# One encoder layer on one core: the per-layer-input product moved into two-bank PSUM tiles, and two norm chains joined into one

## The chip, the cores and the metric

The kernel runs on one core of one Trainium2 chip, as one launch. The metric is device time in microseconds (us) from start to end of an execution, lower is better. The times shown are those of single runs; the profile is one execution recorded by the hardware profiler.

## The reference

One layer of a streaming encoder is computed for 1024 prompt frames and 32 sample frames, in float32. The part that this change touches is the end of the mixing block, the start of the feed-forward block and the per-layer input:

```python
x = x + rms_norm(mix @ w_out, g_post_mix)            # W_out, post-mix norm
hf = rms_norm(x, g_pre_ffn)                          # pre-FFN norm
a, u = split(hf @ w_up, 2)                           # W_up: 1024 x 5632
ffn = (gelu(causal_conv3(a)) * u) @ w_down
x = x + rms_norm(ffn, g_post_ffn)
x = x + (p @ w_ple) * sigmoid(x @ w_ple_gate)        # "ple": p is 256 wide, w_ple 256 x 1024
```

`rms_norm(x, g)` is `x * rsqrt(mean(x*x) + 1e-6) * g` over the 1024 features of a token.

## The kernel before, in words

All 1056 tokens are kept feature-major: 128 partitions hold 128 features, and the tokens lie along the free dimension. In the stages of interest the tokens are cut in four groups of 264 (`H`); groups 0 and 1 are token pair 0, groups 2 and 3 token pair 1. A float32 product is made of three fast products (`product`, L200 to L202): weights and data are each split in a rounded high part and the remainder, and high x high, high x low and low x high are summed in PSUM. ScalarE (ACT) makes the high part with a copy, VectorE (DVE) the low part with a subtraction. A block is one output tile of 128 features x 264 tokens.

The stages around the change, in the order in which TensorE (PE) runs them:

- **W_out** (loop over `p`, then `c`): for each pair, eight output blocks per group, each 24 matmuls. `z_out` copies a finished block out of PSUM and squares it (ACT), and DVE adds the squares into `sqz[g]`. While pair 1 runs, pair 0 is finished beside it: its post-mix norm, its residual sum `x1`, the squares of `x1` (`x1_squares`, L1358 last), and the seven operands of its later products (`build_ops`, L1376 and L1377).
- **ple**: `ple_product` makes 32 blocks of 6 matmuls each (four groups, eight feature blocks `c`). Its PSUM tiles come from `mm_bank`, a ring of six single banks; each block is copied out on ACT (L1420) into an SBUF tile `x4` that takes four blocks, and GpSimd (POOL) issues the store of that tile to `ple_d` (L1422). There are three `x4` buffers, so the first copy into a buffer waits until the store made from it three tiles earlier has landed. Beside the blocks, a table `beside` (filled by `at(m, ...)`) issues pair 1's finishing work: the norm's rows, `x1_sum` on DVE (L1332, L1333), `x1_gain` on ACT (L1339, 16 instructions), operand casts on ACT (L1376) with their low parts on DVE (L1377).
- **up** (`up_unit`, 22 units): products of W_up by a seven-multiplication scheme on 2x2 blocks. Three PSUM tiles `X`, `Y`, `Z` of two banks each (tag `st`, a ring of three in the pool `pf`), one bank per half of the tokens. In unit 0 the two pairs run one after the other, seven steps of 12 matmuls each; the squares of pair 1 (L1362, ACT), their sums (L1367 to L1370, DVE) and its pre-FFN norm lie beside it. In the later units both pairs run in each step. Each step's PSUM result is read by one ACT or DVE operation (L1676 to L1694), and the next step that writes that tile waits for the reading.

A norm is a chain: `sums88` sums the squares over the partitions with tiny matmuls against a column of ones (L1305; three per group, seen as six passes), DVE computes the reciprocal root with a dozen operations on a few columns (`rsqrt`, L211 to L217), `norm_rows` spreads the result back over the partitions with six matmuls (L301, seen as 12 passes), and ACT copies it to `rbT` (L303). Pair 0's pre-FFN chain runs in W_out (sums at `c == 6`, rows after `c == 7`), pair 1's post-mix chain at the start of ple.

The order on each engine is set by the Tile scheduler from the program order, except that `behind(E)` and the like pin an instruction after the last one issued on that engine. Each engine works its own queue strictly in that order. PSUM has eight banks: two for `tr_bank` (tags `tr`) and six that first serve `mm_bank` (pool `pq`) and after ple the pool `pf`.

Of the kernel before, what the change touches and what calls it, by code (L numbers as in the profile page):

```python
# [10 lines left out]
F32 = mybir.dt.float32  # L11
F32R = mybir.dt.float32r
I32 = mybir.dt.int32
AF = mybir.ActivationFunctionType
ALU = mybir.AluOpType
AX = mybir.AxisListType

P = 128
D = 1024
# [3 lines left out]
EPS = 1e-6  # L23
# [7 lines left out]
H = 264  # L31
# [3 lines left out]
T88 = ((0, 88), (88, 88), (176, 88))  # L35
# [24 lines left out]
def layer_kernel(  # L60
# [7 lines left out]
    PSUM = bass.MemoryType.PSUM  # L68
# [9 lines left out]
    def nm(s):  # L78
        n_names[0] += 1
        return f"{s}_{n_names[0]}"  # L80
# [5 lines left out]
    V, S, G, E = nc.vector, nc.scalar, nc.gpsimd, nc.tensor  # L86

    def behind(*engines):

        st = ExitStack()  # L90
        for e in engines:
            ins = next(i for i in reversed(nc.cur_bb.bb.instructions) if i.engine == e.engine)
            st.enter_context(tc.issue_after(ins))
        return st
# [100 lines left out]
    def product(ps, w, wsl, xh, xl, ks, first=True, last=True):  # L195

        for n, (kw, kx) in enumerate(ks):
            wh, wl = w[0][:, kw, wsl], w[1][:, kw, wsl]
            a, b = xh[kx], xl[kx]
            E.matmul(ps, wh, a, start=first and n == 0, stop=False)  # L200
            E.matmul(ps, wh, b, start=False, stop=False)  # L201
            E.matmul(ps, wl, a, start=False, stop=last and n == len(ks) - 1)  # L202
# [1 line left out]
    ALL = slice(0, P)  # L204
    KS = tuple((k, k) for k in range(KT))

    def rsqrt(pool, out, v, n):

        bits = pool.tile([P, n], I32, tag="rsb", name=nm("rsb"), bufs=2)
        t = pool.tile([P, n], F32, tag="rst", name=nm("rst"), bufs=2)  # L210
        V.tensor_scalar(bits[:], v.bitcast(I32), 1, None, op0=ALU.logical_shift_right)  # L211
        V.tensor_scalar(bits[:], bits[:], -1.0, float(0x5F3759DF), op0=ALU.mult, op1=ALU.add)
        y = bits[:].bitcast(F32)
        for _ in range(3):
            V.scalar_tensor_tensor(t[:], y, -0.5, y, op0=ALU.mult, op1=ALU.mult)
            V.tensor_tensor(t[:], t[:], v, op=ALU.mult)
            V.scalar_tensor_tensor(out, t[:], 1.5, y, op0=ALU.add, op1=ALU.mult)  # L217
            y = out
# [19 lines left out]
    def tr_bank():  # L238
        return bank(pp, "tr", 2)
# [56 lines left out]
    def norm_rows(rs, tiles, out):  # L296

        n = sum(m_ for _, m_ in tiles)
        t = tr_bank()
        for i, (c, m_) in enumerate(tiles):  # L300
            E.matmul(t[:, c:c + m_], rs[:m_, i:i + 1].to_broadcast([m_, P]), ident[:m_, :m_],  # L301
                     start=True, stop=True)
        S.copy(out, t[:, :n])  # L303
# [7 lines left out]
    with right("ap") as ap:  # L311
# [210 lines left out]
        with tc.tile_pool(name="np", bufs=1, side="right", reuse_waits="tile") as np_:  # L522
# [103 lines left out]
            xt, rs, rb = ([], [], []), [], []  # L626
# [181 lines left out]
    with right("bp") as bp:  # L808
# [284 lines left out]
        def at(m, f, *a):  # L1093
            small.setdefault(m, []).append(lambda: f(*a))
# [78 lines left out]
    with right("mp") as mp:  # L1173
# [23 lines left out]
        def block(w, wsl, xh, xl, ks, n):  # L1197
            b = mm_bank()
            product(b[:, :n], w, wsl, xh, xl, ks)
            return b  # L1200
# [99 lines left out]
    def sums88(t, g, sq):  # L1300

        for i in range(3):
            o = t[:88, 3 * (g % 2) + i:3 * (g % 2) + i + 1]
            for k, q in enumerate(sq):
                E.matmul(o, q[:, 88 * i:88 * i + 88], ones[:], start=k == 0, stop=k == len(sq) - 1)  # L1305

    def pair_norm(p, scale, t=None, late=False):

        sums = t is None
        t = t or tr_bank()  # L1310
        v = fo.tile([P, 6], F32, tag="nv", name=nm("nv"), bufs=2)
        rs = fo.tile([P, 6], F32, tag="nr", name=nm("nr"), bufs=2)
        V.memset(v[:], 1.0)
        for g in (2 * p, 2 * p + 1) if sums else ():
            sums88(t, g, [sqz[g]])
        V.tensor_scalar(v[:88], t[:88, 0:6], scale, EPS, op0=ALU.mult, op1=ALU.add)
        rsqrt(fo, rs[:], v[:], 6)

        def rows():
            for h in range(2):  # L1320
                o = H * (2 * p + h)
                norm_rows(rs[:, 3 * h:3 * h + 3], T88, rbT[:, o:o + H])
        if sums and not late:
            rows()
        return rows
# [86 lines left out]
    def ple_product(g, beside):  # L1412
        xs = pT.pop(g)
        for c in range(8):
            if c % 4 == 0:
                t = oz.tile([P, 4, H], F32, tag="x4", name=nm("ple"), bufs=3)
            b = block(ple_w[c // 4], slice((c % 4) * P, (c % 4 + 1) * P),
                      [xs[:, 0, k, :] for k in range(2)], [xs[:, 1, k, :] for k in range(2)],
                      ((0, 0), (1, 1)), H)
            S.copy(t[:, c % 4, :], b[:, :H])  # L1420
            if c % 4 == 3:
                gdma(ple_d[:, c - 3:c + 1, H * g:H * g + H], t[:])  # L1422
            for f in beside.pop(8 * g + c, ()):
                f()
# [99 lines left out]
    for p in range(2):  # L1524
        for c in range(8):
            if p and c == 5:
                load_ple()
            w = next_w(2)
            for g in (2 * p, 2 * p + 1):
                z_out(c, g, block(w, ALL, Ra[g], Rb[g], KS, H))  # L1530
                if p == 0 and (c, g) != (0, 0):
                    next(early, None)
            if p == 0:
                if c == 6:
                    x_load(0)
                continue
            if c == 0:
                pair_norm(0, 0.25 / D)
                x1_part(0)
            if c == 1:  # L1540
                x1_squares(0)
                x_load(1)
                x1_part(1)
                op0 = build_ops(0)
            if 2 <= c < 6:
                next(op0)
            if c == 4:
                x1_squares(1)
                p_load(0)
                p_load(1)  # L1550
            if c == 6:
                for _ in op0:
                    pass
                x_load(2)
                x_load(3)
                with behind(E):
                    rows = pair_norm(0, 1.0 / D, late=True)
                p_load(2)
                p_load(3)
            if c == 7:  # L1560
                with behind(E):
                    rows()

    for i in range(4):
        load_part(i)
    rows = pair_norm(1, 0.25 / D, late=True)
    beside = {}

    def at(m, f, *a, on=()):
# [9 lines left out]
        return z[g][:, 4 * i:4 * i + 4, :].bitcast(F32)  # L1579

    b11, b21, b12, b22 = q_rows(2, 0), q_rows(2, 1), q_rows(3, 0), q_rows(3, 1)
    at(6, rows, on=(E,))
    for n, (g, i) in enumerate(((2, 0), (2, 1), (3, 0), (3, 1))):
        at(7, x1_sum, g, i)
        for h in range(2):
# [14 lines left out]
    octx.close()  # L1600
    fctx = ExitStack()
    fp = fctx.enter_context(right("fp"))
    qctx.close()
    qctx = ExitStack()
    pf = qctx.enter_context(tc.tile_pool(name="pf", bufs=1, space=PSUM, reuse_waits="tile"))
    us0 = fp.tile([P, T + 2], F32, tag="a", name="us0", bufs=2)[:, 0:T]
    Sp = page(lq, 3, [P, 4, 2, H], "Sp")
    s1c, U2, nU3, t12 = (Sp[:, i].bitcast(F32) for i in range(4))
# [335 lines left out]
```

## Time and profile before

| | |
|---|---|
| runs | 2012.38, 2012.46 and 2016.8 us; median 2012.46 us |
| profiled execution, span from first to last instruction | 2012.8 us |
| PE busy | 1985.5 us, 99% of the span |
| DVE, ACT, POOL busy | 71%, 48%, 11% |
| TensorE clock, mean of the span | 0.996 of full |

The profiled execution is 0.3 us longer than the median of the runs, so its rows can be set against the runs as they are. In the timeline a row's first number is its start in us from the span's start and the second its duration; matmuls are pipelined, so each is shown for about 0.28 us while the next one starts 0.12 us later. A bracket at a row's end gives how long the engine had been idle and what ended that. W_out's last blocks, ple and unit 0 of up lie between 1150 and 1221 us.

### The profile page before, as it was taken

Reading aid. Unit: us, or ns where it says so; the run is one execution under the profiler, and the core shown is the slowest. Engines: PE = TensorE matmul, PEld = TensorE weight load, DVE = VectorE, ACT = ScalarE, POOL = GpSimd, SP = SyncE. Lnnn points to the kernel's source line nnn. Section 1 sums busy time; section 2 is a strip of 40 time slices with the busy share of each in tenths; the row PEclk is TensorE's granted clock in tenths of the full one; section 3 lists DMA queues with packets and bytes.
Section 4 is the critical chain, followed back from the end, with each engine's and each line's share of the span. In section 5 each row is a group of like instructions: output and inputs, shape, how many; then the busy total and the mean of one; then the engine's idle time right before and its main releaser. Section 6 shows DMA issues by size and latency. Waiting matters only on the chain.

```text
span 2012.8 us, 37342 instructions
## 1 busy us (share of the span) xinstructions
PE 1985.5 (99%) x14282; PEld 1955.1 (97%) x14282; DVE 1433.6 (71%) x3193; ACT 965.6 (48%) x2184; POOL 226.2 (11%) x318
## 2 busy tenths in 40 slices
PE   7999999999999999999999999999999999999998
PEld 6999999999999999999999999999999999999998
DVE  5788888688888888554455778788887884655552
ACT  5655566556666666542124763333333344444432
POOL 2010100000000000002001123332333310000000
PEclk8999999999999999999999999999999999999999
DMA  8322321411111111377558582222222246655542
GB/s 263 96 94 68 115 64 53 144 54 57 37 54 37 54 53 56 118 229 230 165 167 291 164 296 64 85 75 85 68 92 65 88 137 202 214 190 172 167 129 82
DMA packets 250807, 245.31 MB, mean 122 GB/s; under 512 B 13365, under 2 KB 218696, under 8 KB 250629
## 3 DMA queue, kind: packets, MB, share of 16 engines
q1 hardware_dynamic: 242085, 214.92, 34.2%
q0 software_dynamic: 8464, 27.94, 3.9%
q8 instruction: 112, 1.84, 0.4%
q14 instruction: 66, 0.54, 0.1%
q10 hardware_dynamic: 80, 0.07, 0.0%
HBM read 177.56 MB, written 65.32 MB: 121 GB/s over the span
## 4 chain that ended last, share of the span: by engine, by line
PE 85%; DVE 5%; issue 2%; DMA 1%; ACT 1%; POOL 1%; SPq 0%; POOLq 0%; ACTq 0%; DVEq 0%
PE mm L200 13%; PE mm L201 13%; PE mm L202 13%; PE st L1667 7%; PE st L1665 7%; PE st L1666 7%; PE G L839 2%; PE Y L836 2%; PE G L838 2%; PE G L836 2%; PE Y L839 2%; PE Y L838 2%; PE tr L469 1%; PE X L836 1%; PE so L1030 1%
## 5 line engine op out<-in xcount | busy, mean ns | idle before, releaser
L1665 PE MATMUL st<-op,wt 128*128 128x264 f32 x1232 | 349.1, 284 | 3.7 <-ACT ple L1420 2.3
L1667 PE MATMUL st<-op,wt 128*128 128x264 f32 x1232 | 350.2, 284 | 0.0
L1666 PE MATMUL st<-op,wt 128*128 128x264 f32 x1232 | 348.4, 283 | 0.0
L184 DVE TENSOR_TENSOR wl<-wr,wh 128x1024 fp32r<-128x1024 f32 x132 | 161.6, 1225 | 129.3 <-ACT wh L181 115.5
L1665 PEld LDWEIGHTS st<-op,wt 128*128 128x128 f32 x1232 | 231.8, 188 | 4.8 <-ACT ple L1420 2.5
L1666 PEld LDWEIGHTS st<-op,wt 128*128 128x128 f32 x1232 | 232.1, 188 | 0.0
L1667 PEld LDWEIGHTS st<-op,wt 128*128 128x128 f32 x1232 | 231.5, 188 | 0.0
L181 ACT CAST wh<-wr 128x1024 fp32r<-128x1024 f32 x116 | 121.8, 1050 | 200.8 <-PE mm L201 146.5
L200 PE MATMUL mm<-ac,wh 128*128 128x352 f32 x528 | 170.7, 323 | 0.9 <-DVE Sp L1694 0.9
L201 PE MATMUL mm<-ac,wh 128*128 128x352 f32 x528 | 169.1, 320 | 0.0
L202 PE MATMUL mm<-ac,wl 128*128 128x352 f32 x528 | 169.1, 320 | 0.0
L1444 ACT CAST wt<-wu 128x512 fp32r<-128x512 f32 x126 | 77.7, 619 | 188.4 <-POOL ab L1651 93.7
L200 PE MATMUL mm<-La,wh 128*128 128x384 f32 (+1 forms) x504 | 166.2, 330 | 0.3 <-ACT kt L340 0.3
L201 PE MATMUL mm<-Lb,wh 128*128 128x384 f32 (+1 forms) x504 | 162.2, 322 | 0.0
L202 PE MATMUL mm<-La,wl 128*128 128x384 f32 (+1 forms) x504 | 162.2, 322 | 0.0
L200 PE MATMUL mm<-Ra,wh 128*128 128x264 f32 x512 | 145.5, 284 | 0.0
L201 PE MATMUL mm<-Rb,wh 128*128 128x264 f32 x512 | 145.0, 283 | 0.0
L202 PE MATMUL mm<-Ra,wl 128*128 128x264 f32 x512 | 145.0, 283 | 0.0
L1445 DVE TENSOR_TENSOR wt<-wu,wt 128x512 fp32r<-128x512 f32 x126 | 101.2, 806 | 39.7 <-ACT wt L1444 39.7
L453 ACT ACTIVATE sc<-sc,st 128x257 f32<-128x257 f32 (+1 forms) x144 | 69.6, 485 | 74.8 <-DVE st L448 73.6
L200 PEld LDWEIGHTS mm<-ac,wh 128*128 128x128 f32 x528 | 99.0, 188 | 1.2 <-DVE Sp L1694 1.2
L201 PEld LDWEIGHTS mm<-ac,wh 128*128 128x128 f32 x528 | 99.2, 188 | 0.0
(478 smaller groups left out, 5732.6 us busy)
## 6 DMA issues: line engine op xcount, KB each, us to landing
wr<-in_w_down_dram SPq DMA_DIRECT2D x66, 512.0 KB
wu<-in_w_up_dram SPq DMA_DIRECT2D x42, 512.0 KB
wu<-in_w_in_dram SPq DMA_DIRECT2D x32, 512.0 KB
wr<-in_w_in_dram SPq DMA_DIRECT2D x26, 512.0 KB
ac<-act_d SPq DMA_DIRECT2D x66, 176.0 KB
act_d<-Up SPq DMA_DIRECT2D x21, 528.0 KB
wr<-in_w_out_dram SPq DMA_DIRECT2D x16, 512.0 KB
pw_d<-pw POOLq DMA_DIRECT2D x11, 512.0 KB, 5.1
```

The costliest lines, as they stand in the source:

```text
L181: S.copy(hi[:], raw[:])
L184: V.tensor_tensor(lo[:], raw[:], hi[:].bitcast(F32), op=ALU.subtract)
L200: E.matmul(ps, wh, a, start=first and n == 0, stop=False)
L201: E.matmul(ps, wh, b, start=False, stop=False)
L202: E.matmul(ps, wl, a, start=False, stop=last and n == len(ks) - 1)
L836: E.matmul(o, wh, x[0][k], start=first and k == 0, stop=False, skip_group_check=True)
L838: E.matmul(o, wh, x[1][k], start=False, stop=False, skip_group_check=True)
L839: E.matmul(o, wl, x[0][k], start=False, stop=k == 3, skip_group_check=True)
L1445: V.tensor_tensor(t[:, 1], src, t[:, 0].bitcast(F32), op=ALU.subtract)
L1665: E.matmul(o, wh, xh, start=first and k == 0, stop=False, skip_group_check=True)
L1666: E.matmul(o, wh, xl, start=False, stop=False, skip_group_check=True)
L1667: E.matmul(o, wl, xh, start=False, stop=k == 3, skip_group_check=True)
```

## The change

Three things change. The ple product writes into tiles of the pool `pf`, two blocks per two-bank tile, ring of three; `pf` is opened ahead of ple, and the up projection goes on with the same ring. One ACT copy (L1423 in the new numbering) takes two blocks out at a time, 128 x 528 elements. And pair 0's pre-FFN norm is taken out of W_out and joined with pair 1's post-mix norm at the start of ple as one chain on 12 columns, whose two parts get their own scale; the rows of pair 1 come at block 6 and those of pair 0 at block 9. The chain's small tiles have one buffer each instead of two.

```diff
-    def rsqrt(pool, out, v, n):
+    def rsqrt(pool, out, v, n, bufs=2):
...
@@ pair_norm
-        v = fo.tile([P, 6], F32, tag="nv", name=nm("nv"), bufs=2)
-        rs = fo.tile([P, 6], F32, tag="nr", name=nm("nr"), bufs=2)
+        v = fo.tile([P, 6], F32, tag="nv", name=nm("nv"), bufs=1)
+        rs = fo.tile([P, 6], F32, tag="nr", name=nm("nr"), bufs=1)
...
-        rsqrt(fo, rs[:], v[:], 6)
+        rsqrt(fo, rs[:], v[:], 6, 1)
@@ ple_product
-            b = block(ple_w[c // 4], slice((c % 4) * P, (c % 4 + 1) * P),
-                      [xs[:, 0, k, :] for k in range(2)], [xs[:, 1, k, :] for k in range(2)],
-                      ((0, 0), (1, 1)), H)
-            S.copy(t[:, c % 4, :], b[:, :H])
+            if c % 2 == 0:
+                b = pf.tile([P, 2, 512], F32, tag="st", name=nm("st"), bufs=3)
+            product(b[:, c % 2, :H], ple_w[c // 4], slice((c % 4) * P, (c % 4 + 1) * P),
+                    [xs[:, 0, k, :] for k in range(2)], [xs[:, 1, k, :] for k in range(2)],
+                    ((0, 0), (1, 1)))
+            if c % 2:
+                S.copy(t[:, c % 4 - 1:c % 4 + 1, :], b[:, :, :H])
@@ W_out, c == 6 and c == 7 of pair 1
-                with behind(E):
-                    rows = pair_norm(0, 1.0 / D, late=True)
...
-            if c == 7:
-                with behind(E):
-                    rows()
@@ ahead of ple
+    qctx.close()
+    qctx = ExitStack()
+    pf = qctx.enter_context(tc.tile_pool(name="pf", bufs=1, space=PSUM, reuse_waits="tile"))
     for i in range(4):
         load_part(i)
-    rows = pair_norm(1, 0.25 / D, late=True)
+    t = tr_bank()
+    v = fo.tile([P, 12], F32, tag="nv", name="nv2", bufs=1)
+    rs = fo.tile([P, 12], F32, tag="nr", name="nr2", bufs=1)
+    V.memset(v[:], 1.0)
+    for g in (0, 1):
+        sums88(t[:, 6:12], g, [sqz[g]])
+    for g in (2, 3):
+        sums88(t, g, [sqz[g]])
+    for a, sc in ((0, 0.25 / D), (6, 1.0 / D)):
+        V.tensor_scalar(v[:88, a:a + 6], t[:88, a:a + 6], sc, EPS, op0=ALU.mult, op1=ALU.add)
+    rsqrt(fo, rs[:], v[:], 12, 1)
+
+    def rows(p):
+        for h in range(2):
+            o, a = H * (2 * p + h), 6 * (1 - p) + 3 * h
+            norm_rows(rs[:, a:a + 3], T88, rbT[:, o:o + H])
...
-    at(6, rows, on=(E,))
+    at(6, rows, 1, on=(E,))
+    at(9, rows, 0, on=(E,))
```

How the instructions move is shown at three places. The first is PE from the last but one W_out blocks into ple. Before, with `mm_14521` and `mm_14550` the last two W_out blocks, `sq` the squares of pair 0's `x1`, `sqz` those of pair 1's post-mix norm, `pc` and `wq` the ple product's operands:

```order
L202 MATMUL mm_14455<-Ra_12171,wl_14271 128x264
L1305 MATMUL tr_14493<-ones,sq_2287_14104 88x1 x3
L1305 MATMUL tr_14493<-ones,sq_2316_14341 88x1 x3
L200 MATMUL mm_14521<-Ra_12170,wh_14361 128x264
...
L202 MATMUL mm_14550<-Ra_12171,wl_14362 128x264
L301 MATMUL tr_14579<-ident,nr_14495 128x88 x3
L301 MATMUL tr_14584<-ident,nr_14495 128x88 x3
L200 MATMUL mm_14622<-pc_14347,wq_14351 128x264
L201 MATMUL mm_14622<-pc_14347,wq_14351 128x264
L1305 MATMUL tr_14597<-ones,sqz_13375 88x1 x3
L202 MATMUL mm_14622<-pc_14347,wq_14352 128x264
L1305 MATMUL tr_14597<-ones,sqz_13376 88x1 x3
```

And in the change, at the end of W_out and at the two places of the rows:

```order
L1305 MATMUL tr_14567<-ones,sq_2287_14104 88x1 x3
L1305 MATMUL tr_14567<-ones,sq_2316_14341 88x1 x3
L1305 MATMUL tr_14567<-ones,sqz_13375 88x1 x3
L200 MATMUL st_14599<-pc_14347,wq_14351 128x264
...
L1305 MATMUL tr_14567<-ones,sqz_13376 88x1 x3
...
L301 MATMUL tr_14650<-ident,nr_14569 128x88 x3
L301 MATMUL tr_14655<-ident,nr_14569 128x88 x3
...
L301 MATMUL tr_14695<-ident,nr_14569 128x88 x3
L301 MATMUL tr_14700<-ident,nr_14569 128x88 x3
```

All sums now stand between W_out's last block and the first ple block or inside it, and both sets of rows stand inside ple.

The second place is ACT at the end of ple: the copies of the last eight blocks, the operand casts (`op`), and the first reading of unit 0's tile `X` (`Sp`). Before:

```order
L1420 COPY ple_14879<-mm_14880 128x264
L1420 COPY ple_14879<-mm_14888 128x264
L1376 COPY op_14896<-z_13365 128x1056
L1420 COPY ple_14879<-mm_14899 128x264
L1420 COPY ple_14879<-mm_14907 128x264
L1420 COPY ple_14916<-mm_14917 128x264
L1376 COPY op_14875<-z_13365 128x1056
L1420 COPY ple_14916<-mm_14925 128x264
L1420 COPY ple_14916<-mm_14933 128x264
L1420 COPY ple_14916<-mm_14941 128x264
L1676 COPY Sp_14959<-st_14960 128x264
```

And in the change:

```order
L1423 COPY ple_14842<-st_14843 128x528
L1376 COPY op_14857<-z_13365 128x1056
L1423 COPY ple_14842<-st_14860 128x528
L1423 COPY ple_14875<-st_14876 128x528
L1376 COPY op_14838<-z_13365 128x1056
L1423 COPY ple_14875<-st_14890 128x528
L1691 COPY Sp_14910<-st_14911 128x264
```

The casts keep their place among the blocks, eight copies have become four, and the tile `X` (`st_14911`) now follows the last ple tile (`st_14890`) in the same ring.

The third place is DVE in unit 1 of up, where the scheduler came to another order without an edit there: the gelu part of unit 0 (`us`), the parts of the next weights (`wt`), and the reading of unit 1's tile `Y` into `Sp`. Before:

```order
L1445 TENSOR_TENSOR wt_15394<-wu_15200,wt_15394 128x512
L1680 TENSOR_TENSOR ab_15254<-st_15251,rbT 128x2x264
L1626 TENSOR_TENSOR us_14958<-a_15238,us_14958 128x1024
L1627 TENSOR_TENSOR us_14958<-a_15238,us_14958 128x32
L1683 TENSOR_TENSOR Sp_14959<-st_15252,Sp_14959 128x528
```

And in the change, where lines 1680, 1626, 1627 and 1683 have become 1695, 1641, 1642 and 1698:

```order
L1695 TENSOR_TENSOR ab_15205<-st_15202,rbT 128x2x264
L1448 TENSOR_TENSOR wt_15345<-wu_15151,wt_15345 128x512
L1448 TENSOR_TENSOR wt_15373<-wu_15151,wt_15373 128x512
L1698 TENSOR_TENSOR Sp_14910<-st_15203,Sp_14910 128x528
L1641 TENSOR_TENSOR us_14909<-a_15189,us_14909 128x1024
L1642 TENSOR_TENSOR us_14909<-a_15189,us_14909 128x32
```

The reading of `Y` has moved ahead of the two operations on `us`.

More of the change, by code (lines that the diff above doesn't have):

```diff
@@ L205, in layer_kernel @@
     KS = tuple((k, k) for k in range(KT))
-    def rsqrt(pool, out, v, n):
-        bits = pool.tile([P, n], I32, tag="rsb", name=nm("rsb"), bufs=2)
-        t = pool.tile([P, n], F32, tag="rst", name=nm("rst"), bufs=2)
+    def rsqrt(pool, out, v, n, bufs=2):
+        bits = pool.tile([P, n], I32, tag="rsb", name=nm("rsb"), bufs=bufs)
+        t = pool.tile([P, n], F32, tag="rst", name=nm("rst"), bufs=bufs)
         V.tensor_scalar(bits[:], v.bitcast(I32), 1, None, op0=ALU.logical_shift_right)
@@ L1602, in layer_kernel @@
     fp = fctx.enter_context(right("fp"))
-    qctx.close()
-    qctx = ExitStack()
-    pf = qctx.enter_context(tc.tile_pool(name="pf", bufs=1, space=PSUM, reuse_waits="tile"))
     us0 = fp.tile([P, T + 2], F32, tag="a", name="us0", bufs=2)[:, 0:T]
```

## The prediction

> **What bounds the kernel now.** I read the page's first part, then PE's waits, then PE's timeline from the end of W_out to unit 1 of up.
>
> ```profile
> PE 1985.5 (99%) x14282; PEld 1955.1 (97%) x14282; DVE 1433.6 (71%) x3193; ACT 965.6 (48%) x2184; POOL 226.2 (11%) x318
> PE st L1665 <- ACT ple L1420: 2.3, 1, 2.3
> ```
>
> PE is the bound, so the change is worth the PE time that it frees. The largest wait after the start is one of 2.3 us: `X` of unit 0 waits for a ple copy. The timeline shows it with its neighbours.
>
> ```profile
> 1156.65 0.56 PE L1305 MATMUL tr<-ones,sq 128*88 128x1 f32 x6
> 1157.85 0.63 PE L1305 MATMUL tr<-ones,sq 128*88 128x1 f32 x6 [0.64 <-DVE sq L1358]
> 1158.34 0.37 PE L200 MATMUL mm<-Ra,wh 128*128 128x264 f32 x1
> 1158.54 0.29 PE L201 MATMUL mm<-Rb,wh 128*128 128x264 f32 x1
> ...
> 1164.23 1.47 PE L301 MATMUL tr<-ident,nr 88*128 88x88 f32 x12
> ...
> 1165.82 0.56 PE L1305 MATMUL tr<-ones,sqz 128*88 128x1 f32 x6
> 1166.24 0.37 PE L202 MATMUL mm<-pc,wq 128*128 128x264 f32 x1
> ...
> 1166.86 0.37 PE L200 MATMUL mm<-pc,wq 128*128 128x264 f32 x1
> ...
> 1171.70 1.47 PE L301 MATMUL tr<-ident,nr 88*128 88x88 f32 x12
> 1172.95 0.37 PE L200 MATMUL mm<-pc,wq 128*128 128x264 f32 x1
> ...
> 1195.25 0.39 PE L1665 MATMUL st<-op,wt 128*128 128x264 f32 x1 [2.27 <-ACT ple L1420]
> ...
> 1220.82 0.36 PE L1665 MATMUL st<-op,wt 128*128 128x264 f32 x1 [0.28 <-DVE Sp L1694]
> ...
> 1236.57 0.39 PE L1665 MATMUL st<-op,wt 128*128 128x264 f32 x1 [0.99 <-DVE Sp L1683]
> ```
>
> Six passes of L1305 take 0.42 (1165.82 to 1166.24), twelve of L301 take 1.25 (1171.70 to 1172.95). A restart after tiny matmuls costs 0.08 (0.20 to the next one at 1158.34, instead of 0.12). From 1166.86 to 1171.70 stand 39 matmuls (three left of block 0, six blocks of six) and one restart: 0.122 each, 0.73 a block. X starts at 1195.25, unit 1 at 1220.82. Why that second stretch is long shows in stretches of 3.41 us; the columns are length, then PE, PEld, DVE, ACT and POOL busy, then the granted clock.
>
> ```profile
> 35.63:39.04 3.41, 2.30 (x12) 1.48 (x11) 2.98 (x6) 3.34 (x7) 2.17 (x4) 1.00 0.44 146
> 39.04:42.45 3.41, 3.41 (x11) 1.87 (x9) 2.30 (x11) 2.23 (x6) 2.21 (x6) 0.50 0.91 264
> 45.87:49.28 3.41, 3.41 (x12) 2.92 (x11) 1.50 (x6) 0.00 (x0) 0.00 (x0) 0.50 0.80 88
> 1155.20:1158.61 3.41, 2.77 (x28) 2.69 (x27) 3.41 (x8) 1.06 (x4) 1.32 (x2) 1.00 0.62 194
> 1192.75:1196.16 3.41, 1.14 (x9) 0.93 (x9) 2.89 (x3) 2.19 (x5) 1.00 (x2) 1.00 0.97 356
> 1196.16:1199.57 3.41, 3.41 (x18) 3.41 (x17) 0.00 (x0) 2.01 (x3) 0.36 (x1) 0.50 1.04 382
> ```
>
> The wait leaves a stretch in which PE is busy for 1.14, and the next 3.41 us run at half clock: a further loss of 1.7. [...]
>
> ACT makes X wait. It works without a pause through ple's second half, as its timeline shows:
>
> ```profile
> 1176.89 0.38 ACT L1420 COPY ple<-mm 128x264 f32<-128x264 f32 x1 [0.35 <-PE mm L202]
> 1177.17 0.92 ACT L1339 ACTIVATE z<-x,gvec 128x264 f32<-128x264 f32 x2
> 1177.99 0.37 ACT L1420 COPY ple<-mm 128x264 f32<-128x264 f32 x1
> ...
> 1181.51 1.09 ACT L1376 CAST op<-z 128x1056 fp32r<-128x1056 f32 x1
> ...
> 1193.28 0.38 ACT L1420 COPY ple<-mm 128x264 f32<-128x264 f32 x1 [0.97 <-DMA ple_d<-ple]
> ...
> 1197.84 4.01 ACT L1362 ACTIVATE x<-x 128x1056 f32<-128x1056 f32 x4
> ...
> 1224.00 0.60 ACT L1676 COPY Sp<-st 128x528 f32<-128x528 f32 x1 [2.07 <-DVE ab L1620]
> ```
>
> To the next start a copy takes 0.28, two gains 0.82, a cast 0.98 (1.09 less the 0.1 of overlap seen on a copy). At 1193.28 ACT is held by a store, and the copies behind it free X.
>
> **The change part by part.** I follow PE through the new order.
>
> *End of W_out.* The first sums leave it: 1.69 (1156.65 to 1158.34, 0.64 of it idle) and the restart 0.08. The rows at 1164.23 leave too, so W_out ends at 1164.23 − 1.77 = 1162.46. Eighteen passes of sums follow, 1.26; ple starts at 1163.72.
>
> *Ple without waits.* 32 blocks 23.4, six passes with restart 0.5, two sets of rows 2 × 1.33 = 2.66, one restart 0.08: PE would end at 1190.4. The joined chain costs DVE a dozen operations less; 12 columns instead of 6 I take at the same price. It is out of PE's way: 5.1 us of blocks lie between sums and rows.
>
> *Copies.* The nearest row for a 528-element copy is the same shape from the same kind of tile, 0.60 at 1224.00, so 0.50 to the next start against 2 × 0.28: next to nothing saved. I take 0.50; the ends are 0.45 and 0.56 for two.
>
> *ACT's queue.* The gains wait for DVE's `x1_sum`:
>
> ```profile
> 1172.94 2.43 DVE L1332 TENSOR_TENSOR z<-z,rbT 128x1056 f32<-128x1056 f32 x2 [3.53 <-ACT rbT L303]
> 1175.29 2.42 DVE L1333 TENSOR_TENSOR x<-x,z 128x1056 f32<-128x1056 f32 x2
> ```
>
> They follow the rows of block 6, which move from 1171.70 to 1169.3, so the first is ready at 1174.2, ahead of ACT. Number the two-block tiles 0 to 15. Tile 5 is complete at 1175.8; from its copy (done 1176.5) ACT is saturated: four gains and a copy are 2.14, giving tile 6 at 1178.6 and 7 at 1180.75; two casts and a copy, tile 8 at 1183.2; gains again, 9 at 1185.3 and 10 at 1187.5; a cast, 11 at 1188.9; 12 at 1189.4; a cast, 13 at 1190.9.
>
> *New waits.* PE may start tile n when tile n−3 is copied. Tile 11 is due at 1183.1 (wait 0.1 to 0.2), 12 at 1184.8 (wait 0.6), 13 at 1187.0 (wait 0.6), 14 needs none; with 0.1 for each restart 1.7 in all. X is due at 1190.4 + 1.7 = 1192.1 and needs only tile 13's copy, 1190.9. **Gain at X: 1195.25 − 1192.1 = 3.15.** Bounds: none of these waits (a gain of 4.9), or 0.7 at all five tiles from 11 on (1.4).
>
> *Held store.* Tile 14's copy needs the store of tiles 8 and 9:
>
> ```profile
> 1186.60 0.75 POOL L1422 DMA_DIRECT2D ple_d<-ple  x1 [2.42 <-ACT ple L1420]
> DMA to landing us min/median/max: 3.4/6.6/8.4
> ```
>
> Issued at 1185.3 it lands at 1191.9 by the median; tile 14 is copied at 1192.4, `Y` is due at 1193.6. Behind that copy wait a cast (1193.4), tile 15 (1193.9, `Z` due at 1195.0), X's reading (1194.2) and the four squares, 1.0 each, to 1198.2.
>
> *Unit 0.* 168 matmuls 20.5, twelve passes of sums 0.9, rows 1.3: 22.7 without waits or half clock, where the trace has 25.57. New waits come from DVE's sums of squares, which the new order puts ahead of readings that PE needs:
>
> ```profile
> 1200.41 1.25 DVE L1367 TENSOR_TENSOR x<-x 128x1056 f32<-128x1056 f32 x1
> 1201.70 0.71 DVE L1368 TENSOR_TENSOR x<-x 128x528 f32<-128x528 f32 x1
> ```
>
> From the last squares (1198.2) DVE needs about 3.5 us (one L1367 and L1368, three operations of 0.43, the rest of the other group's sums) up to the reading of Z: 1201.7, where PE stands at 1200.9. The next reading of Y follows a low part (1.2): 1203.6 against 1203.3. With restarts I take 1.4; the ends are 0 and 2.5. **Gain: 25.57 − 22.7 − 1.4 = 1.45.**
>
> *Unit 1.* There PE waits 0.99 for the reading of Y, which stood behind the gelu product:
>
> ```profile
> 1234.58 1.22 DVE L1626 TENSOR_TENSOR us<-a,us 128x1024 f32<-128x1024 f32 x1 [1.09 <-ACT a L1624]
> ...
> 1235.82 0.70 DVE L1683 TENSOR_TENSOR Sp<-st,Sp 128x528 f32<-128x528 f32 x1
> ```
>
> Put ahead of it, the reading is done some 2 us sooner. **Gain: 0.99 + 0.1 = 1.1**; what is late next there, the weight parts, DVE clears before it.
>
> *At nothing.* The single buffers reorder a few copies early in W_out; PE has no gap there:
>
> ```profile
> 1068.00:1120.00 52.00, 52.00 (x438) 52.00 (x436) 25.95 (x39) 26.87 (x54) 7.39 (x13) 1.00 0.83 271
> ```
>
> ACT and DVE are half busy, so a shift of a copy or two is covered; without cover it would cost a copy, 1.1. SP's queue is unchanged; on POOL one store passes one load. From unit 2 on nothing differs.
>
> Sum: 3.15 + 1.45 + 1.1 = 5.7. The span, 2012.8, is 0.3 above the median of the runs, 2012.46; 2012.46 − 5.7 = **2006.8 us**, 0.28% less. A measurement of this kernel tells about 0.3%, 6.0 us, from no change, so the forecast lies just inside.
>
> **The rivals.**
> *The tile waits stay away* (0.15): they are 0.1 to 0.6 each, and ACT a little quicker per tile closes them. For: the saturated stretch is only 15 us. Against: a row bounds every piece. With them gone, 2006.8 − 1.7 = 2005.1.
>
> *Half clock in ple* (0.09): the waits at tiles 12 and 13 leave about 2.0 of 3.41 us busy, near the 2.30 after which the clock fell at 39.04, below the 2.77 at which it held. One stretch costs 1.7: 2008.5. [...]
>
> *The store holds ACT, or X still waits for the last copy* (0.07): a landing of 8.4 puts squares and readings 1.8 later; waiting for tile 15 would cost X 1.9. Either gives 2008.6.
>
> *Slower* (0.04): the clock stays down as from 39.04 to 49.28, three stretches, 5.1 us. It decides if PE is under 2.3 of 3.41 busy at the tile waits, again at unit 0's waits, and at the sums: three times 5.1 less 5.7 is +9.6, 2022.1; twice would be 2017. Against: matmuls fill those stretches, where small transposes did at 39.04.
>
> **How the numbers follow.** Forecast 0.65, spread about ±1, so the 6.0 line cuts it nearly in half: 0.32 beyond it. Faster by over 0.3%: 0.32 + 0.15 = 0.47. Within 0.3%: 0.33 + 0.09 + 0.07 + 0.01 (clock down twice) = 0.50. Slower: 0.03. The range goes from 2004.4 (tile waits and half of unit 0's gone) to 2010.2 (half clock and held store together); outside are the slower case and the outermost bounds.
>
> **What would show it.** X starts without a wait on a ple copy, and no half clock stands there; PE idles for ple copies three times, 0.1 to 0.6, at tiles 11 to 13; ACT's first pause in ple's second half is for the store; PE waits about 1 us for Z's reading in unit 0; the wait in unit 1 is gone. A half-clock stretch in ple, or waits above 2 us in unit 0, would prove it wrong.

## The result, and the profile after

| | runs | median us | ratio to before, 95% interval |
|---|---|---|---|
| the kernel changed, first set | 9 | 2008.60 (2007.17 to 2010.64) | 0.9980 (0.9971 to 0.9988) |
| the same kernel, second set | 12 | 2009.91 (2006.52 to 2014.6) | 0.9993 (0.9984 to 1.0003) |

The forecast was 2006.8 us, 5.7 less than before, in a range of 2004.4 to 2010.2. The first set is 3.9 us below before (2012.46 in that set too), the second 1.6 (2011.48). The two traces of each kernel, compared stage by stage below, put the change itself at 2.5 us, of which about half comes from two events that one trace of before shows each and the other doesn't. The direction was forecast, with more than twice the size.

The first part of the page of after: PE is still busy for 99% of a shorter span.

```profile
PE 1981.8 (99%) x14282; PEld 1952.6 (97%) x14282; DVE 1432.7 (71%) x3181; ACT 964.3 (48%) x2168; POOL 223.0 (11%) x318
```

The span, 2007.4 us, is 5.4 shorter, but 3.5 of this was won before the change begins: the first tiny sums of W_out (L1305) start at 1115.58 here, at 1119.10 in before. I count from there. PE's timeline of after, from those sums to unit 2 of up:

```profile
1115.58 1.03 PE L1305 MATMUL tr<-ones,sqz 128*88 128x1 f32 x12
...
1153.94 0.39 PE L202 MATMUL mm<-Ra,wl 128*128 128x264 f32 x1 [0.41 <-DVE wl L184]
...
1160.97 0.37 PE L200 MATMUL st<-pc,wq 128*128 128x264 f32 x1
...
1182.64 0.39 PE L200 MATMUL st<-pc,wq 128*128 128x264 f32 x1 [0.39 <-ACT ple L1423]
...
1184.76 0.39 PE L200 MATMUL st<-pc,wq 128*128 128x264 f32 x1 [0.39 <-ACT ple L1423]
...
1189.27 0.28 PE L1680 MATMUL st<-op,wt 128*128 128x264 f32 x1
...
1199.08 0.39 PE L1680 MATMUL st<-op,wt 128*128 128x264 f32 x1 [0.79 <-DVE us L1700]
...
1213.59 0.28 PE L1680 MATMUL st<-op,wt 128*128 128x264 f32 x1
...
1229.37 0.39 PE L1680 MATMUL st<-op,wt 128*128 128x264 f32 x1 [0.72 <-DVE Sp L1698]
1232.93 0.39 PE L1680 MATMUL st<-op,wt 128*128 128x264 f32 x1 [0.39 <-DVE Up L1700]
...
1242.39 0.39 PE L1680 MATMUL st<-op,wt 128*128 128x264 f32 x1 [0.49 <-ACT Sp L1691]
1246.24 0.39 PE L1680 MATMUL st<-op,wt 128*128 128x264 f32 x1 [0.65 <-DVE Sp L1693]
```

X (1189.27) starts without a wait. Ple has the two waits of 0.39 forecast for its late tiles, unit 0 the one of 0.79 for the reading of Z. Not forecast are the wait in W_out for a weight's low part (0.41), and four waits in units 1 and 2 of up, of which before had one (0.99).

The table gives the stages in every trace, from differences of start times on PE: from the first sums to X; units 0, 1 and 2 (168 matmuls each, counted off); the first product of the down projection to the first sums there (L1257); and the first sums of W_out to the span's end. From unit 3 to the down projection it is 386.6 in all of them (387.1 in the last), and from the sums there to the end 270.6 to 271.2. So these five stages hold nearly the whole difference. The expectations quoted below count "X to unit 3" up to the 37th matmul of unit 3, 4.36 us more than the columns units 0 to 2 add up to.

| kernel | to X | unit 0 | unit 1 | unit 2 | down | first sums to end |
|---|---|---|---|---|---|---|
| before | 76.15 | 25.57 | 21.69 | 20.35 | 92.75 | 893.70 |
| before, again | 76.58 | 24.41 | 21.68 | 20.35 | 94.13 | 894.31 |
| after | 73.69 | 24.32 | 22.35 | 22.05 | 92.16 | 891.82 |
| after, again | 73.60 | 24.39 | 21.76 | 22.04 | 92.16 | 891.16 |
| tiles alone | 74.16 | 25.31 | 21.74 | 22.08 | 91.58 | 892.12 |
| norm chain alone | 75.05 | 24.42 | 21.68 | 20.35 | 92.69 | 891.43 |
| after, single copies | 77.45 | 25.89 | 21.67 | 20.35 | 92.15 | 894.75 |
| after, GpSimd held (no effect) | 73.96 | 24.35 | 22.39 | 22.05 | 92.16 | 892.10 |
| after, GpSimd waits | 73.87 | 24.33 | 21.96 | 21.03 | 92.15 | 890.54 |
| after, sums on DVE | 73.97 | 24.32 | 20.35 | 20.34 | 92.16 | 888.34 |
| before, sums on DVE | 76.13 | 24.43 | 20.44 | 20.35 | 93.16 | 891.79 |
| norm chain, one pad | 74.97 | 24.41 | 21.68 | 20.34 | 92.16 | 890.82 |
| after, two pads | 74.15 | 24.31 | 22.39 | 22.03 | 92.61 | 893.24 |
| after, sums on DVE, again | 74.10 | 24.31 | 20.35 | 20.34 | 91.62 | 888.67 |

### The profile page after: what moved, and what is told of

It reads as the page before. It is cut to its first block, busy times and chain, and to the rows that moved or that the text cites. A ratio compares the mean times of both kernels' runs of the same rounds, so it can differ in the third digit from the quotient of the medians.

```text
span 2007.4 us, 37311 instructions
## 1 busy us (share of the span) xinstructions
PE 1981.8 (99%) x14282; PEld 1952.6 (97%) x14282; DVE 1432.7 (71%) x3181; ACT 964.3 (48%) x2168; POOL 223.0 (11%) x318
## 4 chain that ended last, share of the span: by engine, by line
PE 86%; DVE 6%; ACT 2%; issue 1%; DMA 1%; POOL 0%; ACTq 0%; DVEq 0%; POOLq 0%
PE mm L200 13%; PE mm L202 13%; PE mm L201 13%; PE st L1682 7%; PE st L1681 7%; PE st L1680 7%; PE G L839 2%; PE Y L836 2%; PE G L838 2%; PE G L836 2%; PE Y L839 2%; PE Y L838 2%; PE tr L469 1%; PE X L836 1%; PE so L1030 1%
## 5 line engine op out<-in xcount | busy, mean ns | idle before, releaser
L200 PE MATMUL mm<-ac,wh 128*128 128x352 f32 x528 | 170.6, 323 | 0.0
L202 PE MATMUL mm<-ac,wl 128*128 128x352 f32 x528 | 169.7, 321 | 0.0
L200 PE MATMUL mm<-La,wh 128*128 128x384 f32 (+1 forms) x504 | 166.5, 331 | 0.3 <-ACT kt L340 0.3
L202 PE MATMUL mm<-La,wl 128*128 128x384 f32 (+1 forms) x504 | 162.4, 322 | 0.0
L202 PE MATMUL mm<-Ra,wl 128*128 128x264 f32 x512 | 145.1, 283 | 0.4 <-DVE wl L184 0.4
L200 PE MATMUL mm<-Ra,wh 128*128 128x264 f32 x512 | 145.4, 284 | 0.0
L202 PEld LDWEIGHTS mm<-ac,wl 128*128 128x128 f32 x528 | 99.4, 188 | 0.0
L201 PEld LDWEIGHTS mm<-ac,wh 128*128 128x128 f32 x528 | 99.3, 188 | 0.0
```

## The experiments

**Both kernels again, for a second trace.** No edit.

> The kernel before, unchanged, for a second trace of it. Theory A (the change moves only the stretch from the end of W_out to unit 2 of up, and the 3.5 us by which the trace of after is already ahead at the first sums of W_out, 1115.58 against 1119.10, came from the clock at the start of the run): the same time within 0.1%; the first sums of W_out stand anywhere from 1115 to 1119, X of unit 0 again waits 2.0 to 2.5 us for a ple copy, and the stretch from the first sums of W_out to the end of unit 2 is as long as in the first trace within 0.5 us, save the half clock behind X's wait, which costs 1.7 or nothing. Theory B (the head start of after belongs to the change): the first sums stand at 1119.1 again, within 0.3 us.

> The changed kernel, unchanged, for a second trace of it. Theory A: about 4 us less than before in time; the first sums of W_out stand anywhere from 1115 to 1119; from there to the end of unit 2 it is shorter than the kernel before by 1.3 (both with the half clock behind X's wait in before) and the waits in units 1 and 2 of up (0.72, 0.39, 0.49, 0.65) come again. Theory B: the first sums stand at 1115.6 again, within 0.3 us, and the gain is made before W_out.

Before took 2012.11 us (ratio 1.0003, 0.9993 to 1.0013), after 2009.91 as above, so 1.6 less than before in that set and not the 4 expected. The first sums stood at 1114.59 and 1113.64: the head start of after was chance. It follows the granted clock of the first 70 us, as two answers of the windows view show (columns as in the prediction): after again, and the slowest start but one, the last kernel of the table.

```profile
0.00:70.00 70.00, 57.77 (x336) 50.32 (x337) 49.56 (x143) 44.44 (x95) 15.21 (x38) 1.00 0.71 214
```

```profile
0.00:70.00 70.00, 56.13 (x291) 47.32 (x292) 45.60 (x134) 39.45 (x82) 15.25 (x38) 0.90 0.72 210
```

Over the 14 traces the first sums stand at 1113.6 to 1115.4 with a clock of 1.00, 1114.9 to 1116.4 with 0.98, 1118.8 and 1118.9 with 0.95, and 1119.1 to 1122.7 with 0.93 or 0.90. This is up to 9 us, most of it with the clock (the two traces at 0.93 stand 3.6 apart). Before's own medians, over the sets of these runs, lie between 2010.92 and 2012.46, so a timing can be off by a microsecond or two, and a stage table decides what it can't.

The half clock behind X's wait was chance as well. Before again, PE's timeline and the stretch behind it:

```profile
1191.17 0.39 PE L1665 MATMUL st<-op,wt 128*128 128x264 f32 x1 [2.17 <-ACT ple L1420]
```

```profile
1191.20:1194.60 3.40, 3.40 (x28) 3.40 (x29) 0.80 (x2) 1.87 (x4) 0.75 (x1) 1.00 1.03 404
```

X waits 2.17 us and the clock stays at 1.00; in the kernel before with sums on DVE (below) it waits 2.14 and unit 0 takes 24.43. Of these three traces only the first has 25.57.

**The two halves of the change, each alone.**

```diff
 # tiles alone: before, with the pool pf opened ahead of ple, and
+            if c % 2:
+                S.copy(t[:, c % 4 - 1:c % 4 + 1, :], b[:, :, :H])
 # norm chain alone: after, with before's
+            S.copy(t[:, c % 4, :], b[:, :H])
```

> The kernel before with the two-bank tiles and the pair copies alone; both norm chains stay where they were. Theory A (X was freed by needing only tile 13's copy): X waits under 0.5 us and no half clock follows; X starts 2 to 3 us sooner behind the first sums of W_out than in before (76.15 there), and the time is 2 to 3 us below before. Rival (the gain comes from the earlier rows, which let ACT's gains begin 1.5 us sooner): X still waits over 1 us, and the time is within 1 us of before.

> The changed kernel with the ple product in single-bank tiles, copied block by block, as before; the joined norm chain alone is new. Theory A: X needs the last ple copies again and waits 1 to 2.5 us for them; the 1.3 us that PE saves at the end of W_out are waited out there, and the time is within 1 us of before. Rival (the rows 1.5 us sooner let ACT finish sooner): X waits under 1 us, no half clock, and the time is 2 to 3 us below before.

Tiles alone took 2010.26 us (0.9995, 0.9986 to 1.0004), the norm chain alone 2008.79 (0.9987, 0.9979 to 0.9996); the 2 to 3 us expected of the tiles are not in the time. Against the mean of the two traces of before, X comes 2.2 us sooner with the tiles, 1.3 with the chain and 2.7 with both. But what the tiles win at X is gone by unit 3: units 0 to 2 take 69.1 against 66.4 in before again. The chain keeps its 1.3, and alone it brings as much as both halves together: 891.43 from the first sums to the end, against 891.16 and 891.82. The expectation that the chain's saving would be waited out at X was wrong: X's wait falls from 2.17 to 0.99.

Why only the tiles lose it again shows in unit 0, in an order that nobody edited, a fourth place beside the three shown for the change. PE starts unit 1 at the same point with either half, 99.47 us behind the first sums. But with the chain alone the tiny sums of pair 1's pre-FFN norm (L1305) stand behind 100 of unit 0's 168 matmuls, as in before, and with the tiles behind 120. DVE's part of that norm waits for them (0.73 us in before, 1.48 with the tiles), and its last product of unit 0 (L1637 in one kernel, L1628 in the other) starts 1.71 us into unit 1 with the chain alone, 3.47 with the tiles. PE's and DVE's timelines, the chain alone first:

```profile
1203.46 1.03 PE L1305 MATMUL tr<-ones,sq 128*88 128x1 f32 x12
1216.55 1.25 DVE L1637 TENSOR_TENSOR us<-us,rbT 128x1056 f32<-128x1056 f32 x1
```

```profile
1206.22 1.03 PE L1305 MATMUL tr<-ones,sq 128*88 128x1 f32 x12
1217.82 1.25 DVE L1628 TENSOR_TENSOR us<-us,rbT 128x1056 f32<-128x1056 f32 x1
```

The 14 traces fall in two groups by this. In six the sums stand behind 100 matmuls, DVE's product starts 1.7 us into unit 1, and unit 2 takes 20.34 or 20.35. In eight, after among them, the numbers are 120 and 3.5 to 4.6, and unit 2 takes 22.0 to 22.1 except where, below, GpSimd's sums really wait or go to DVE. No run changes this order alone.

**Single copies from the two-bank tiles.**

```diff
-            if c % 2:
-                S.copy(t[:, c % 4 - 1:c % 4 + 1, :], b[:, :, :H])
+            S.copy(t[:, c % 4, :], b[:, c % 2, :H])
```

> The changed kernel with the two-bank tiles kept and each block copied by itself (two copies of 264 elements for one of 528). By the step of the prediction that costed the pair copy at 0.50 against 2 x 0.28: X starts within 0.4 us of after (73.6 behind the first sums of W_out), and the waits of ple (two of 0.39) grow by at most 0.2 each. Rival (the pair copy is what lets ACT keep up): the waits of ple double or more, and X starts over 1 us later.

The rival held, by one profiled execution: X starts 3.8 us later than in after, with one ple tile still to come behind it. PE's waits, and ACT's timeline at the end of ple:

```profile
PE st L200 <- ACT ple L1422: 2.1, 5, 0.6
```

```profile
1187.86 0.94 ACT L1422 COPY ple<-st 128x264 f32<-128x264 f32 x3
1189.32 0.38 ACT L1422 COPY ple<-st 128x264 f32<-128x264 f32 x1 [0.52 <-PE st L202]
1190.04 0.38 ACT L1422 COPY ple<-st 128x264 f32<-128x264 f32 x1 [0.34 <-PE st L202]
1190.32 2.05 ACT L1376 CAST op<-z 128x1056 fp32r<-128x1056 f32 x2
1192.27 0.94 ACT L1422 COPY ple<-st 128x264 f32<-128x264 f32 x3
```

The pair copy saves ACT hardly any time, as forecast (0.48 to the next start for two times 0.28). From the first sums to the end it is worth 3 us all the same. With single copies PE and ACT wait for each other by turns, and two casts, 2.05 us together, stand ahead of the last three copies. How much of it is the halves and how much the new order of the queue, this run can't separate.

**Units 1 and 2: GpSimd's sums beside DVE.** In after, GpSimd makes the weight sums of unit 2 (L1454 to L1456) while DVE finishes unit 0. POOL's timeline and DVE's of after:

```profile
1216.74 1.43 POOL L1454 TENSOR_TENSOR sa<-wu 128x512 f32<-128x512 f32 x1 [17.41 <-PE st L1682]
1218.25 2.29 POOL L1455 TENSOR_TENSOR wu<-wu,wu 128x512 f32<-128x512 f32 x1
...
1239.09 1.30 POOL L1454 TENSOR_TENSOR sa<-wu 128x512 f32<-128x512 f32 x1 [8.96 <-PE st L1682]
1240.46 1.29 POOL L1455 TENSOR_TENSOR wu<-wu,wu 128x512 f32<-128x512 f32 x1
```

```profile
1216.94 1.28 DVE L1716 TENSOR_TENSOR ab<-Sp,rbT 128x32 f32<-128x32 f32 x1
1218.14 1.25 DVE L1640 TENSOR_TENSOR us<-us,rbT 128x1056 f32<-128x1056 f32 x1
1219.31 1.25 DVE L1632 COPY tails<-ab 128x2 f32<-128x2 f32 x1
1220.48 0.16 DVE L1633 COPY tails<-ab 128x2 f32<-128x2 f32 x1
...
1239.13 1.28 DVE L1632 COPY tails<-ab 128x2 f32<-128x2 f32 x1
...
1241.89 2.33 DVE L1637 SCALAR_TENSOR_TENSOR a<-ab,cvec,a 128x1058 f32<-128x1058 f32 x1 [1.34 <-ACT a L1636]
```

A copy of two columns takes 1.25 us where its twin right behind takes 0.16, and it ends with POOL's sum: 1219.31 + 1.25 = 1220.56, 1218.25 + 2.29 = 1220.54. So does the 32-column product (1218.22 against 1218.17), which takes 0.19 in before. In before, the same copies stand just ahead of the sums:

```profile
1223.69 0.17 DVE L1617 COPY tails<-ab 128x2 f32<-128x2 f32 x1
```

```profile
1224.06 2.89 POOL L1451 TENSOR_TENSOR sa<-wu 128x512 f32<-128x512 f32 x1 [20.71 <-DVE ab L1620]
1227.03 2.19 POOL L1452 TENSOR_TENSOR wu<-wu,wu 128x512 f32<-128x512 f32 x1
1229.30 2.19 POOL L1453 TENSOR_TENSOR wu<-wu,sa 128x512 f32<-128x512 f32 x1
```

The sums start 3.15 to 3.25 us behind the start of unit 1 in both kernels. What moved against them is DVE, by the new order in unit 0: its last product of unit 0 (L1625, L1640) starts 1.7 us behind that point in before (1222.53 against 1220.82), 4.55 in after and 3.5 in after again. The first attempt to keep the two apart pinned the first sum behind DVE's copies in the order of issue:

> The changed kernel, with the first of GpSimd's weight sums for units 2 and 3 of up held until DVE has made its three two-column copies for the unit before (the copies of tails and of the cache columns). Theory A (in after these sums start while DVE still reads and copies, and DVE's instructions beside them take 1.2 to 2.3 us where they took 0.16 to 1.3, which makes the late readings of units 1 and 2): the copies take 0.16 again, the two waits of unit 2 (0.49 and 0.65) go and those of unit 1 shrink, and the stretch from X to unit 3 falls from 72.6 to 73.1 us to 70.8 to 71.5. Rival (DVE is behind PE because PE no longer waits in unit 0, and GpSimd has no part in it): the waits stay, and the stretch stays within 0.3 of 72.6 to 73.1.

It tells nothing on the theory. GpSimd started its sums as early as in after, and the copy beside them took as long; the pin had set no wait between the engines (2010.23 us, 0.9989, 0.9979 to 0.9999). POOL's second sum and DVE's first copy:

```profile
1219.39 2.29 POOL L1456 TENSOR_TENSOR wu<-wu,wu 128x512 f32<-128x512 f32 x1
```

```profile
1220.45 1.25 DVE L1633 COPY tails<-ab 128x2 f32<-128x2 f32 x1
```

The second made a true wait of it, by data:

```diff
+        if u in (2, 3):
+            G.tensor_copy(s1[:, 0, 0:2], abs_[u - 2][:, 1026:1028])
         adder.tensor_tensor(s1, a21, a22, op=ALU.add)
```

> The changed kernel, in which GpSimd first copies the two cache columns of the unit before into the tile of its first weight sum, for units 2 and 3 of up: the sum is overwritten over them, so it really starts only when DVE has made its three small copies (the hold tried before set an order only, and GpSimd still started 3 us ahead of them). Theory A (DVE's instructions beside GpSimd's sums are the long ones): DVE's copies take 0.16 instead of 1.25, GpSimd starts 1 to 2 us later than in after behind the start of unit 1, the waits of unit 2 (0.48 and 0.69) go, and from X to unit 3 it takes 70.8 to 71.8 us instead of 72.6 to 73.1. Rival (DVE is behind PE there whatever GpSimd does, because PE waits less in unit 0): the waits of unit 2 stay within 0.3 of their sum and the stretch takes 72.3 or more.

The copies take 0.16, and of unit 2's two waits one is left (0.41). Those of unit 1 (0.72 and 0.38) stay, so the copies are not the whole of it. Units 0 to 2 take 67.3, or 71.7 in the count of the expectation, inside its span. The median is 2007.81 us (0.9982, 0.9973 to 0.9991). DVE's row and POOL's rows:

```profile
1216.69 0.16 DVE L1635 COPY tails<-ab 128x2 f32<-128x2 f32 x1
```

```profile
1217.21 1.02 POOL L1455 COPY sa<-ab 128x2 f32<-128x2 f32 x1 [19.16 <-DVE ab L1638]
1218.32 1.29 POOL L1456 TENSOR_TENSOR sa<-wu 128x512 f32<-128x512 f32 x1
```

The third takes GpSimd out of it, at 2.5 us more work for DVE in each unit:

```diff
-        adder = V if u < 2 else G
+        adder = V if u < 4 else G
```

> The changed kernel with the weight sums of units 2 and 3 of up made by DVE instead of GpSimd: four operations of 0.62 more in each unit on DVE, none beside GpSimd. Theory A: no DVE instruction there is longer than 1.4 us, the small copies take 0.16, and in spite of 2.5 us more work a unit the waits of unit 2 are no longer than in after (1.2 in all). Rival: DVE, already late, falls back by all of that, and the waits of units 1 and 2 grow to 3 us or more in all (2.1 to 2.3 in after).

All four waits are gone, although DVE's last product still starts 3.47 us into unit 1, and units 1 and 2 take 20.35 and 20.34, the time of a unit in which PE never waits. PE's waits for up and ple, all that are left:

```profile
PE st L1680 <- DVE us L1700: 0.8, 1, 0.8
PE st L200 <- ACT ple L1423: 0.8, 2, 0.4
```

The same edit in the kernel before:

> The kernel before with the weight sums of units 2 and 3 of up made by DVE instead of GpSimd, and nothing else. Theory A (unit 1's wait of 0.99 in before has the same cause as the waits of units 1 and 2 in after, GpSimd's sums beside DVE, and not DVE's order as the prediction had it): the wait of 0.99 goes, from X to unit 3 it takes 69.3 to 69.8 us (70.8 in before without half clock), and from the first sums of W_out to the end about 1.2 less than before, 892.5 to 893.0. Rival (the wait is DVE's order, the gelu product ahead of the reading): the wait stays at 0.7 or more.

Its wait of 0.99 in unit 1 is gone (20.44), and the time is 2009.78 us (0.9984, 0.9974 to 0.9993). So that wait, too, was due to GpSimd's sums: in before ACT's next weight cast waits for the third of them, which ends at 1231.49 (the releaser named is a memset of 0.10 right behind it).

```profile
1231.52 0.62 ACT L1444 CAST wt<-wu 128x512 fp32r<-128x512 f32 x1 [5.75 <-POOL ab L1651]
```

Behind that cast stand the gelu, DVE's product with it, and the reading of Y. Both engines lose: in before, POOL's three sums took 2.89, 2.19 and 2.19, where one that goes ahead of DVE takes 1.3. The first of them began just behind three weight parts of DVE:

```profile
1223.90 1.90 DVE L1445 TENSOR_TENSOR wt<-wu,wt 128x512 fp32r<-128x512 f32 x3
```

The rows above show the delay both ways round: in after a tiny copy that comes second ends with GpSimd's sum (1220.56 and 1220.54), and a sum that comes second ends 1.15 us behind DVE, at 1220.54 in after (the product of L1640 ended at 1219.39) and at 1226.95 in before (the three weight parts ended at 1225.80). What makes one wait for the other no run here shows.

**The down projection: which banks the last Z stands in.** PE waits about 1 us at its start in both traces of before and with the norm chain alone, never in after. Extra tiles, each written once by ACT, turn the ring of three:

```diff
+    pad = pf.tile([P, 2, 512], F32, tag="st", name="pad", bufs=3)
+    S.copy(pad[:, 0, 0:1], ones[:])
```

> The kernel with the joined norm chain alone (ple in single banks), and one extra two-bank tile in the pool of up, written once by ACT behind the last ple copies, so that X, Y and Z of unit 0 take the next pair of banks. Theory A (X waits for the last copies only because it takes the banks of the last two ple blocks; and the wait of 0.9 to 1.1 at the first product of the down projection goes with the pair of banks that the last Z stands in, which the 16 ple tiles moved by one): X's wait falls from 0.99 to under 0.3, the wait at the down projection goes, and from the first sums of W_out to the end it is 1.5 to 2 shorter than with the joined chain alone (891.4), 889.5 to 890. Rival (PE ahead of DVE by as much meets late readings in units 1 and 2, as in after): X starts sooner, and units 1 and 2 give 1.5 or more of it back.

> The changed kernel with two extra tiles in the pool of ple and up, so that every later tile stands two pairs of banks further, as before the change. Theory A (the pair of banks): the wait of about 0.9 us at the start of the down projection comes back, and nothing else between W_out and the down projection differs by more than 0.3 us. Rival (that wait went for another reason, such as PE's earlier time): no wait there.

With one pad the chain-alone kernel loses the wait (down 92.16; 2008.47 us, 0.9986, 0.9974 to 0.9997); with two pads in after, by one profiled execution, it comes back (the rest of that expectation missed: X stands 0.5 later too, with a wait of 0.86 in W_out). Before, and after with two pads:

```profile
1651.51 0.43 PE L200 MATMUL mm<-ac,wh 128*128 128x352 f32 x1 [0.94 <-DVE Sp L1694]
```

```profile
1654.06 0.43 PE L200 MATMUL mm<-ac,wh 128*128 128x352 f32 x1 [0.81 <-DVE Sp L1713]
```

Sixteen ple tiles move a ring of three by one place: the wait goes and comes with that place, and has nothing to do with the work of ple. What it is worth is less clear. It puts the stage's 13th matmul 1.1 to 1.4 us later (3.13 us behind the first in before, 1.92 in after), but the pads changed the whole stage by only 0.53 and 0.45. For behind it the matmuls follow each other at one of three paces, kept through the stage (from the 200th to the 500th): 0.1589 us in before, with the chain alone, with two pads and with the tiles alone, which have no such wait, 0.1600 in after and with one pad, 0.1611 in before again, all at a granted clock of 1.00. What sets the pace no run here shows.

The other half of the expectation failed, and with it 1 us of the 1.5 to 2 expected: X waited 1.27 for the pad's copy, which stands behind ACT's last work.

**The version to which this points**, the change with the sums of units 2 and 3 on DVE, timed:

> The changed kernel with the weight sums of units 2 and 3 on DVE, again, now timed: the version to which the experiments point. Theory A: no wait in units 1 and 2; from X to unit 3 69.2 to 69.6 us, from the first sums of W_out to the end 888 to 888.8, so 5 to 6 us less than before by the trace; the median 5 to 6 us under before, 0.25 to 0.3%. Rival (the look before was a lucky one): the waits are back in part, and the time is within 1 us of after's 2008.6 to 2009.9.

2005.68 us (2005.04 to 2011.5, seven runs), ratio 0.9965 (0.9952 to 0.9978). By the table it is 5.5 us below before and 3.0 below after; after was not run in this set, and the medians stand 6.7 apart, more than the 5 to 6 expected. Its profiled execution had the clock of 0.90 at the start, shown above.

## Why the prediction was right, and where its steps failed

The time fell in the range and on the forecast side, in part by luck: the gain at X came out, those of units 0 and 1 did not, and two stages that it put at nothing moved by 1.7 and by 0.6 or more. By its steps, against both traces of before and after:

- **End of W_out: failed by 0.7.** The sums and rows left W_out as forecast, but they had been the cover of a late weight part. DVE starts it at the same point in both kernels, 37.1 us behind the first sums, and ends it 1.2 us later. After, then before:

```profile
1152.67 1.21 DVE L184 TENSOR_TENSOR wl<-wr,wh 128x1024 fp32r<-128x1024 f32 x1
```

```profile
1156.22 1.23 DVE L184 TENSOR_TENSOR wl<-wr,wh 128x1024 fp32r<-128x1024 f32 x1
```

In before PE sat in its sums then; in after it waits, 0.32 to 0.97 over the kernels with that order. The prediction did not ask what was late next.
- **Ple: right.** From ple's start to X 28.30 us against 28.4, with waits of 0.39 at the two tiles where 0.6 was forecast, no half clock, no wait at X. The gain at X is 2.5 by the first pair of traces and 3.0 by the second, against 3.15.
- **Held store: failed, at no cost.** ACT was to idle about 1 us for the store ahead of tile 14. It does not idle there in after, and for 0.15 us in after again.
- **The rival of half clock in ple: one reading was wrong, and its limit was an estimate.** It set ple's matmuls against small transposes from 39.04 on; about two thirds of PE's time at half clock there went to matmuls of 384 columns (L200 to L202). That a stretch with PE busy for less than 2.30 of 3.41 us brings half clock was an estimate from two rows (2.30 and 2.77), and before again speaks against it: around its wait of 2.17 PE is busy for at most 1.24 of 3.41 us, and the clock stays at 1.00. Nothing came to hang on either.
- **The pair copy at next to nothing: right by ACT's time, wrong in what it decides** (about 3 us, single copies).
- **Unit 0: right in length (24.1 forecast, 24.3 and 24.4 measured), wrong in the gain.** The 25.57 it was set against held a half-clock stretch that two other traces with such a wait (2.17 and 2.14 us) lack. Against 24.41, which has a wait of 0.55 instead, the gain is 0.1, not 1.45.
- **Unit 1: failed.** The reading did move ahead of the gelu product, but the wait hung on GpSimd's sums. Instead of a gain of 1.1 there is a loss of 0.1 to 0.7.
- **"From unit 2 on nothing differs": failed twice.** Unit 2 loses 1.7: the tiny sums of unit 0 stand 20 matmuls later, DVE comes later into unit 1, and its small copies fall under GpSimd's sums. That the sums beside DVE cost the time is shown (moved to DVE, the loss is gone); that DVE is late by the order in unit 0 is a comparison of traces. The down projection gains 0.6 or more by the ring's place. Both lie where no instruction of the stage was changed.

Sum by the means of the two pairs of traces: −2.7 at X, −0.6 in unit 0 (the half clock, in one trace of two), +0.4 in unit 1, +1.7 in unit 2, −1.3 in the down projection: −2.5. (There the second trace of before is 1.4 longer than the first with a wait only 0.12 longer; the slower pace, 0.1611 for 0.1589 over 576 matmuls, is 1.3 of it.) Without the half clock of the one trace and the slow pace of the other, about 1.3 is left, as much as the norm chain keeps alone. That the first set of runs showed 3.9 is chance on top of it.

## What to carry to other kernels

When PE is given time in one stage, follow the gain through the next two, and compare the order of the instructions there as well: the scheduler had moved tiny sums in a unit that nobody edited, and DVE came late behind them (3.5 to 4.6 us into unit 1 instead of 1.7). Before a stall of the profile is counted as a gain, take a second trace: here half clock followed X's wait of 2.1 to 2.3 us in one trace of three. And where two engines' operations end at the same moment, move the work of one to the other and time that; here more work on the busier engine took units 1 and 2 from 44.40 to 40.69 us.

## What the runs showed of the hardware

- DVE copies of 128 x 2 elements took 1.25 to 1.28 us when they began during a GpSimd sum, more than 0.1 us before its end, and 0.15 to 0.18 otherwise. GpSimd's sums took up to 2.9 us beside DVE, and 1.3 where they went first. I had taken GpSimd, 11% busy, for harmless.
- A wait of 2.1 to 2.3 us on PE was followed by half clock in one trace of three: 3.41 us at 0.50 behind the wait of 2.27, none behind those of 2.17 and 2.14.
- The first 70 us ran at a mean clock of 0.90 to 1.00 from run to run, and W_out's first sums stood up to 9 us apart over the 14 traces (4.5 in two of the same kernel).
- The down projection's matmuls of 352 columns kept one of three paces through the stage, 0.1589, 0.1600 or 0.1611 us, at the same granted clock.
